# One encoder layer for two request groups on one core: a head by channel quarters, a gate in column tiles, a balance that paces the filler, and split weights kept in DRAM

## The chip, the cores and the metric

The kernel runs on one NeuronCore of a Trainium2 chip. The metric is the device time of one execution in microseconds; "the time" is the median of several executions. A profiled execution is one more, taken by the hardware profiler, and its trace is what the views below show. The engines are PE (TensorE, matmuls; PEld is its loading of weights), DVE (VectorE), ACT (ScalarE), POOL (GpSimd) and SP, which here issues all DMAs in order.

## What is computed

Two groups (prompt and sample) of 1024 tokens by 1024 channels go through the same layer with the same weights:

```python
mod = silu(c) @ w_ada + b_ada
shift, scale, gate = split(mod, 3)
h = rms_norm(x, norm_g) * (1 + scale) + shift
qa, ka, va, za, qb, kb, vb, zb, ga, gb = split(h @ w_in)
oa = gqa_attention(rope(rms_norm(qa)), rope(rms_norm(ka)), va) * silu(za)
ob = diff_attention(rope(rms_norm(qb)), rope(rms_norm(kb)), vb, lam)
ob = rms_norm(ob, subln_g) * (1 - lam_init) * silu(zb)
merged = sigmoid(ga) * (oa @ w_proj_a) + sigmoid(gb) * (ob @ w_proj_b)
y = x + gate * (merged @ w_out)
```

Branch A has 8 query heads on 2 key heads of 64; branch B has 4 heads with two 64-wide softmax maps each. Everything is float32.

## The kernel before

**Precision.** Most matmuls run in the fast float32r form. To keep accuracy each operand is split into a high part (a rounded copy, made by ACT) and a low part (the residual, made by DVE), and three products are summed: high-high, high-low, low-high. For a weight tile `split_w` (L175) does this, called by `load_w` (L186, lines L178 and L179 per quarter) and in `load_w_proj` (L220, L221). `load_w` brings a tile of 1024 x 256 in four DMAs of 256 KB into three rotating buffers and splits each into one of two weight buffers (`wpool`). Both groups load and split all 21 column tiles of `w_in` anew, 84 quarters per group.

**Head of group one.** `start` (L337) loads the adaLN weights (8 tiles of 1 MB, `load_ada`), x transposed in two halves of 512 tokens (`load_xT0`), and the weights of ka and va. `ada` (L292) multiplies the two conditioning vectors (2 columns as weights) with 512 columns of adaLN weights, 64 records of L298 in all; `ada_end` turns the result with small transposes into columns `modc`. `squares`, `added`, `inv_rms` and `spread` (L251 to L288) make the root-mean-square factors; `modulated` (L317) scales, shifts and splits x into `ht`, first for channels 0 to 3, then 4 to 7. `start_late` (L368) does the second half of the tokens. Then `head` (L1020) weaves `kva_gen` and `qa_gen` (projections through `proj_tt`, L506, 24 matmuls of 256 columns each at L515) with z steps.

**Fillers.** `z_gen` (L693) makes the gates of both branches and the merge gates: 12 items a group, each four tiles of 24 matmuls of 512 columns (L704), each tile three steps. Their result goes to DRAM (`zd`, L715). These steps depend on `ht` alone and fill TensorE while attention waits on other engines.

**Attention.** 32 units of branch A, then 16 of branch B, each for 256 queries: scores on PE (L737, L738), maximum on DVE (L739), exponential on ACT (L741), a flip by DVE's 32 x 32 transpose (L774) and four DMAs (L779), a split (L787, L788), and the product with the values (L799, L800 for A, L839 for B). For B the second map is scaled by a factor from a reciprocal (L760) on DVE and a product on POOL (L761). In `rows` (L523) the normalisation of q and k has a small addition on DVE (L532) and a power on POOL (L533).

**Order.** Python generators yield after each step, and `weave` (L71) runs several of them by shares: each stream has a number of steps and a lead, and the one whose done share less its lead is smallest goes next. `phase` (L1115) weaves one part of attention with the projections that the next part needs and with a fixed number of z steps (`Z_SHARE`, `ATT_W`, `IN_A`, `Z_A`, tables of constants). Tile's scheduler then fixes each engine's order with its own model of time, with attention at a raised priority; the kernel's engines run these orders.

**End of a group.** The last attention head (h = 3) is woven with `fill` (gate columns by `gate_gen`, L445, in group one; leftover z steps; part of `merge_gen`) and with `gated_gen` (L912), which multiplies attention by its gates and norm factors. For branch B the factors are spread by PE transposes of a broadcast column (L942). `merge_gen` (L954) projects both branches, `out_gen` (L992) makes the output; in group one the next group's `ht_gen` runs beside it.

Of the kernel before, what the change touches and what calls it, by code (L numbers as in the profile page):

```python
# [20 lines left out]
P = 128  # L21
# [15 lines left out]
Z_SHARE = (  # L37
    (7, 19, 6, 3, 2, 4),
    (9, 14, 7, 3, 2, 6),
)  # L40
Z_HEAD = (6, 5)
Z_HEAD_A = (-0.4, -0.45)
ATT_W = (
    (1.07, 0.933, 1.1, 0.95, 1.129, 1.52),
    (1.15, 1.354, 1.035, 1.196, 0.85, 1.069),
)
IN_A = (
    (0.1, -0.05, 0.2, 0.05, 0.15, 0.1),
    (0.1, -0.05, 0.45, 0.25, 0.15, 0.65),
)  # L50
Z_A = (
    (0.1, 0.0, 0.4, -0.05, -0.2, 0.0),
    (0.15, 0.05, 0.35, 0.15, -0.3, -0.2),
)
LAST_ATT = 44
LAST_FILL = 26
GATED_A = -0.3
TAIL = 5
TAIL_A = 0.3
LAG = 2  # L60

# [20 lines left out]
def drain(*gens):  # L82
    for g in gens:
        if g is not None:
            for _ in g:
                pass


@with_exitstack
def kernel(ctx: ExitStack, tc: tile.TileContext, t: dict):  # L90
# [26 lines left out]
    alone = [True]  # L117
    turn = [0]

    def gbank():  # L120
        turn[0] += 1
        if alone[0] and turn[0] % 5 in (0, 2):
            return sbank()[:, :512]
        return fbank()
# [33 lines left out]
    dma = nc.sync.dma_start  # L158
    x_sample = t["x_sample"][0]
# [12 lines left out]
    nc.vector.memset(nhalf, -0.5)  # L172


    def split_w(w, q, st):  # L175
        wh = w[:, q * 2 : q * 2 + 2, 0, :]
        wl = w[:, q * 2 : q * 2 + 2, 1, :]
# [3 lines left out]
    def split_early(what):  # L181
        w, sts = what
        for q, st in enumerate(sts):
            split_w(w, q, st)

    def load_w(pieces, early=False):  # L186

        w = wpool.tile([P, NCH, 2, 256], F32R, tag="w", name=nm("w"))
        sts = []
        for q in range(4):  # L190
            if early:
                if q % 2 == 0:
                    room = halves2(ptile())
                st = room[q % 2].rearrange("p (c n) -> p c n", c=2)
# [4 lines left out]
            for src in pieces(q):  # L199
                n = src.shape[1]  # L200
                dma(st[:, :, off : off + n], src.rearrange("(c p) n -> p c n", p=P))
# [4 lines left out]
        return (w, sts) if early else w  # L206

    def w_cols(mat, *cols):
        def pieces(q):
            return [mat[q * 256 : (q + 1) * 256, c : c + n] for c, n in cols]  # L210
        return pieces

    def load_w_proj(br, half):

        w = wpool.tile([P, 4, 2, 512], F32R, tag="w", name=nm("w"))
        mat = t["w_proj_b" if br else "w_proj_a"][0]
        for c in range(4):
# [3 lines left out]
            nc.vector.tensor_tensor(out=w[:, c, 1, :], in0=st, in1=w[:, c, 0, :].bitcast(F32), op=ALU.subtract)  # L221
        return w
# [990 lines left out]
```

## Time and profile before

| | |
|---|---|
| median of 3 runs | 1942.35 us (1939.26 to 1943.64) |
| the profiled execution's own time | 1933.24 us |
| its span, first to last instruction | 1931.5 us |
| PE / DVE / ACT / POOL busy | 1881.2 / 1397.3 / 991.7 / 414.7 us |
| DMA moved | 295.25 MB, mean 153 GB/s |

In the views, "PE" rows are matmuls, and float32 (not float32r) matmuls stand as two records each. A row of the timeline has start, length, engine, line, operation, tiles, shapes and count; in brackets stands the idle time before it with what ended it. In the rows of the stretches a number in brackets is a count. Rows of groups have busy us and the mean ns of one, then the idle time before them. PE's busy time is longer than its work where matmuls are not back to back, so a share near 100% does not mean full pace.

### The profile page before, as it was taken

To read this page: it belongs to the slowest core of one execution; us is meant where nothing else is said; L and a number is where in the kernel's file an instruction comes from. 1 tells how busy PE (TensorE), PEld (TensorE's weight loads), DVE (VectorE), ACT (ScalarE), POOL (GpSimd) and SP (SyncE) were. 2 spreads that over 40 slices of the span, in tenths; PEclk is the share of its full clock that TensorE was granted. 3 is DMA by queue.
4 is the path that set the end of the run, shared out by engine and by line. 5 is a ranking of instruction groups with operands and counts; after the bars stand their busy time and mean duration, and the time that the engine had idled before them with its cause. 6 is when DMAs were issued, how large, how long until landed. Compare 5 with 4: busy or idle time off the path is not lost.

```text
span 1931.5 us, 30797 instructions
## 1 busy us (share of the span) xinstructions
PE 1881.2 (97%) x10466; PEld 1610.0 (83%) x10466; DVE 1397.3 (72%) x2145; ACT 991.7 (51%) x2091; POOL 414.7 (21%) x758
## 2 busy tenths in 40 slices
PE   8899999999999999999999999999989999999999
PEld 3788888888988995778889888898877989888887
DVE  5669886778898677767465788688788767777731
ACT  4446665666666454414233566566666545542310
POOL 1342300120335051000124231013221524201000
PEclk9999999999999999999999999999999999999999
DMA  9125465556554436875641455565545343477522
GB/s 319 45 81 146 135 173 148 153 148 176 152 142 110 116 92 192 273 256 181 218 140 39 137 144 166 145 172 151 154 129 162 107 113 100 143 234 264 180 104 77
DMA packets 271613, 295.25 MB, mean 153 GB/s; under 512 B 37857, under 2 KB 220257, under 8 KB 271457
## 3 DMA queue, kind: packets, MB, share of 16 engines
q1 hardware_dynamic: 271456, 293.28, 51.4%
q8 instruction: 84, 1.38, 0.3%
q14 instruction: 73, 0.59, 0.1%
HBM read 133.72 MB, written 42.01 MB: 91 GB/s over the span
## 4 chain that ended last, share of the span: by engine, by line
PE 81%; DVE 7%; DMA 5%; issue 2%; ACT 2%; SPq 1%; POOL 1%; DVEq 0%; ACTq 0%; POOLq 0%
PE f L704 22%; PE f L515 19%; PE f L1007 5%; PE s L737 5%; PE a L839 5%; PE s L738 5%; PE f L976 4%; PE s L1007 4%; PE a L800 3%; PE a L799 3%; PE s L976 2%; DMA q<-p 2%; DVE m L739 2%; DVE p L774 1%; PE f L298 1%
## 5 line engine op out<-in xcount | busy, mean ns | idle before, releaser
L704 PE MATMUL f<-u,w 128*128 128x512 f32 x2232 | 574.2, 395 | 2.0 <-DVE ssB L863 1.5
L515 PE MATMUL f<-w,u 128*128 128x256 f32 x3456 | 487.5, 285 | 7.5 <-DVE u L571 3.7
L515 PEld LDWEIGHTS f<-w,u 128*128 128x128 f32 x3456 | 457.8, 190 | 29.0 <-DVE u L571 4.3
L704 PEld LDWEIGHTS f<-u,w 128*128 128x128 f32 x2232 | 404.2, 188 | 77.8 <-DVE ssB L863 1.8
L739 DVE TENSOR_REDUCE m<-s 128x1 f32<-128x1024 f32 x256 | 311.0, 1217 | 51.3 <-PE s L738 48.4
L774 DVE STREAM_TRANSPOSE p<-p 128x1024 f32<-128x1024 f32 x192 | 238.3, 1241 | 92.7 <-ACT p L741 89.3
L738 PE MATMUL s<-u,sw 128*128 128x512 f32 x512 | 203.8, 398 | 0.0
L788 DVE TENSOR_TENSOR q<-q,hi 128x512 fp32r<-128x512 f32 x256 | 171.5, 690 | 34.3 <-ACT hi L787 32.3
L787 ACT ACTIVATE hi<-q 128x512 fp32r<-128x512 f32 x256 | 153.6, 624 | 76.2 <-DMA q<-p 37.8
L741 ACT ACTIVATE p<-s,m,rsA 128x1024 f32<-128x1024 f32 x128 | 153.8, 1202 | 71.4 <-DMA q<-p 69.6
L178 ACT ACTIVATE w<-st 128x512 fp32r<-128x512 f32 x196 | 114.4, 625 | 99.2 <-DMA st<-in_w_in_dram 42.4
L741 ACT ACTIVATE p<-s,m,rsB 128x1024 f32<-128x1024 f32 x128 | 154.3, 1205 | 6.5 <-DMA q<-p 1.9
L179 DVE TENSOR_TENSOR w<-st,w 128x512 fp32r<-128x512 f32 x196 | 132.8, 706 | 34.2 <-ACT w L178 33.1
L658 POOL TENSOR_TENSOR row<-row,gB 128x96 f32<-128x96 f32 x64 | 33.8, 528 | 485.7 <-ACT row L529 474.1
L799 PE MATMUL a<-hi,u 128*128 128x256 f32 x512 | 132.2, 284 | 2.8 <-DMA q<-p 1.8
L800 PE MATMUL a<-q,u 128*128 128x256 f32 x512 | 129.3, 286 | 2.6 <-DVE q L788 2.6
L976 PE MATMUL f<-u,w 128*128 128x512 f32 x540 | 130.5, 393 | 1.3 <-DVE u L987 1.3
L839 PE MATMUL a<-q,u 128*128 128x256 f32 x512 | 127.1, 385 | 3.9 <-DVE oo L816 3.0
L976 PEld LDWEIGHTS f<-u,w 128*128 128x128 f32 x540 | 100.5, 188 | 23.0 <-DVE u L987 2.3
L839 PEld LDWEIGHTS a<-q,u 128*128 128x128 f32 x512 | 95.6, 193 | 20.0 <-DVE oo L816 3.6
L737 PE MATMUL s<-u 128*128 128x512 f32 x256 | 108.3, 424 | 3.3 <-ACT p L741 3.2
L737 PE MATMUL s<-u,u 128*128 128x512 f32 x256 | 102.4, 400 | 8.5 <-ACT p L741 3.1
(181 smaller groups left out, 2557.5 us busy)
## 6 DMA issues: line engine op xcount, KB each, us to landing
q<-p SPq DMA_DIRECT2D x768, 128.0 KB, 2.6
st<-in_w_in_dram SPq DMA_DIRECT2D x132, 256.0 KB, 3.1
zd<-ev SPq DMA_DIRECT2D x96, 256.0 KB, 2.2
sw<-u SPq DMA_DIRECT2D x256, 64.0 KB, 2.1
p<-zd SPq DMA_DIRECT2D x64, 256.0 KB, 3.7
u<-in_w_ada_dram SPq DMA_DIRECT2D x8, 1024.0 KB, 10.4
st<-in_w_in_dram SPq DMA_DIRECT2D x64, 128.0 KB, 2.8
st<-in_w_out_dram SPq DMA_DIRECT2D x32, 256.0 KB, 3.6
```

What stands on the lines that cost most here:

```text
L515: nc.tensor.matmul(ps, lt[c][:, sl], w[:, c, wi, :], start=(k == 0), stop=(k == 23))
L704: nc.tensor.matmul(ps, w[:, c, wi, e * P : (e + 1) * P], rt[c], start=(k == 0), stop=(k == 23),)
L737: nc.tensor.matmul(s[:, sl], q, k[:, sl], start=True, stop=False)
L738: nc.tensor.matmul(s[:, sl], sw, k[:, sl], start=False, stop=True)
L739: nc.vector.tensor_reduce(out=m, in_=s, axis=AX.X, op=ALU.max, negate=True)
L741: nc.scalar.activation(pt.rearrange("p (j c a) -> p j c a", j=4, c=8), s.rearrange("p (c a j) -> p j c a", c=8, j=4), AF.Exp, scale=rs, bi ...
L774: nc.vector.transpose(pt, pt)
L799: nc.tensor.matmul(acc, lt, th[:, c, :], start=(k == 0), stop=False)
L800: nc.tensor.matmul(acc, lt, tl[:, c, :], start=False, stop=(k == 7))
L839: nc.tensor.matmul(acc, u["v"][:, k], pT[:, k], start=(k == 0), stop=(k == 7))
L976: nc.tensor.matmul(ps, w[:, c, wi, d * P : (d + 1) * P], o[:, oi, :], start=(k == 0), stop=(k == 11))
L1007: nc.tensor.matmul(ps, w[:, c, wi, e * P : (e + 1) * P], m[:, mi, :], start=(k == 0), stop=(k == 23))
```

## The change

1. **Head by channel quarters.** x comes first; each adaLN tile pair holds shift and scale of 256 channels. `ada` uses four column positions of the array, 32 wide, one for each of four channel chunks, so that four partial sums stand in four strips of 32 partitions; `ada_sum` adds them with a small matmul. As soon as a quarter of the channels is modulated, its products for ka and va (`kva_early`) and for the first two z tiles (`z_one`) are accumulated, over the first 512 tokens, in four halves of PSUM banks and two banks that stay open. `act`, `vec`, `pe` and `dma_next` keep these instructions in the program's order. `z_first` goes on with four z tiles, the second half by chunks; `proj_tt` takes the finished tiles from `given`.
2. **Gate.** `gate_gen` works by four column tiles of 256, in the same strips, and stands behind the head's qa projection instead of in the last attention stretch.
3. **Pacing.** `phase` no longer weaves by shares. It keeps an account: each step has a cost on PE and on DVE, and the account grows by DVE's cost less PACE times PE's. At or below zero attention goes next; above it a projection step or a z step. No z shares are set per phase.
4. **Kept weights.** After group one has split a quarter of a `w_in` tile, `keep` stores high and low parts to DRAM (512 KB), and group two loads them with `again` straight into the weight buffer. `w_proj_a` likewise; `w_proj_b` and `w_out` are split as before.
5. **Small moves.** The addition at L532 goes to POOL; the reciprocal at L760 becomes a power on POOL; the copy at L855 goes to ACT; branch B's norm factors go through DRAM (`rB`) and come back broadcast, instead of by PE transposes.
6. **Constants** for the head and the last stretch (`Z_HEAD`, `LAST_ATT`, `LAST_FILL`, `TAIL` and their leads).

```diff
+PACE = (
+    (1.15, 0.95, 1.0, 1.0, 1.0),
+    (0.95, 0.95, 1.05, 1.0, 1.02),
+)
+EARLY = (
+    (1.2, 1.05, 1.35, 1.22, 1.22),
+    (1.2, 1.1, 1.2, 1.23, 1.15),
+)
+A_STEP, B_STEP, F_STEP, Z_STEP = (0.47, 1.01), (0.68, 0.98), (0.79, 0.65), (1.82, 0.35)
...
+    def keep(key, q, w):
+
+        kept[key, q] = dpool.tile([P, 1024], F32, name=nm("kept"))
+        dma(kept[key, q].rearrange("p (c s n) -> p c s n", c=2, s=2), w[q].bitcast(F32))
+
+    def again(key, q, w):
+        dma(w[q].bitcast(F32), kept[key, q].rearrange("p (c s n) -> p c s n", c=2, s=2))
...
         for q in range(4):
+            if (key, q) in kept:
+                again(key, q, w)
+                continue
...
             if not early:
                 split_w(w, q, st)
-        return (w, sts) if early else w
+                if pieces.of is w_in:
+                    keep(key, q, w)
...
+    def ada(wts, cpad):
+
+        acc = gbank()
+        for q, wt in enumerate(wts):
+            for c in range(4):
+                pe.matmul(
+                    acc[32 * c : 32 * c + 32], cpad[:, q * 4 + c], wt[:, c], start=(q == 0), stop=(q == 1),
+                    tile_position=(0, 32 * c),
+                )
...
+        rs = inv_rms(added(squares(xT[0])))
...
+        rsb = spread(rs)
+        early.update(kva=[x for b in two_banks() for x in (b[:, :256], b[:, 256:])], z=two_banks())
+        ps = ada_sum(ada(wts[:2], cpad))
+        for quarter in range(4):
+            cs = range(quarter * 2, quarter * 2 + 2)
+            by_rms(xT[0], cs, rsb)
+            split_early(kva_w[0][1], quarter)
+            ada_end(quarter, ps)
...
+            split_early(kva_w[1][1], quarter, act)
+            modulated(ht, 0, xT[0], cs)
+            split_early(kva_w[1][1], quarter, vec)
+            for c in cs:
+                kva_early(ht, c)
+            part = ada(wts[quarter * 2 + 2 : quarter * 2 + 4], cpad) if quarter < 3 else None
+            for c in cs:
+                for e in range(2):
+                    z_one(ht, 0, c, kva_w[1][0], e, early["z"][e], pe)
...
     def gate_gen():
...
+        for n in range(4):
+            acc = gbank()[:, :256]
+            nc.vector.memset(acc, 0.0)
...
+                        nc.tensor.matmul(
+                            acc[32 * c : 32 * c + 2], cT[:, q * 4 + c], st[:, j], start=(q == 0), stop=(q == 1),
+                            tile_position=(0, 32 * c),
+                        )
...
-        nc.vector.tensor_scalar(out=ss, in0=ss, scalar1=EPS, scalar2=None, op0=ALU.add)
+        nc.gpsimd.tensor_scalar(out=ss, in0=ss, scalar1=EPS, scalar2=1.0, op0=ALU.add, op1=ALU.mult)
...
-            nc.vector.reciprocal(f, su)
+            nc.gpsimd.tensor_tensor(out=f, in0=su, in1=mone, op=ALU.pow)
...
-        nc.vector.tensor_copy(query_order(o), piece_order(acc))
+        nc.scalar.activation(query_order(o), piece_order(acc), AF.Copy)
...
-                rb = gbank()
-                for k in range(4):
-                    r = st["ssB"][:, e - 4, hf * 4 + k : hf * 4 + k + 1]
-                    nc.tensor.transpose(rb[:, k * P : (k + 1) * P], r.to_broadcast([P, P]), ident)
+                dma(rb, rB[e % 2, hf].partition_broadcast(P))
...
+            drain(islice(zs, 6))
+            late()
+            weave((kva, 27, 0.0), (islice(zs, Z_FIRST[0]), Z_FIRST[0], Z_FIRST_A[0]))
+            weave((qa, 27, 0.0), (islice(zs, Z_FIRST[1]), Z_FIRST[1], Z_FIRST_A[1]), (gate_gen(), 8, GATE_A))
...
+        def phase(k, *fs):
+
+            n_att, att_cost = (16 * (6 + PV_LAG), A_STEP) if k < 2 else (4 * (9 + PV_LAG), B_STEP)
+            fs, n_fs = chain(*fs), 31 * len(fs)
+            done, seen, live, fs_live, z_live = 0, 0, True, True, True
+            while live or fs_live:
+                cost = None
+                if live and ahead[0] <= 0.0:
+                    live = next(att) is None
+                    seen += 1
+                    cost = att_cost if live else (0.0, 0.0)
+                elif fs_live and (not live or not z_live or done * n_att < n_fs * EARLY[g][k] * seen):
+                    fs_live = next(fs, None) is not None
+                    done += 1
+                    cost = F_STEP
+                elif z_live:
+                    z_live = next(zs, None) is not None
+                    cost = Z_STEP
+                else:
+                    live = live and next(att) is None
+                    seen += 1
+                    cost = att_cost
+                ahead[0] += cost[1] - PACE[g][k] * cost[0]
...
-            if g == 0:
-                yield from gate_gen()
             yield from zs
             drain(first)
-            yield from islice(merge, 16 - TAIL)
+            yield from islice(merge, 16 - TAIL[g])
```

More of the change, by code (lines that the diff above doesn't have):

```diff
@@ L117 @@
     alone = [True]
+    early = {}
     turn = [0]
@@ L121, in gbank @@
         turn[0] += 1
-        if alone[0] and turn[0] % 5 in (0, 2):
+        if alone[0] and not early and turn[0] % 5 in (0, 2):
             return sbank()[:, :512]
@@ L1040, in new_state @@
         st["rA"] = dpool.tile([64, P], F32, name=nm("rA"))
+        st["rB"] = [dpool.tile([16, P], F32, name=nm("rB")) for _ in range(2)]
         st["od"] = [
```

379 lines of the change are left out of this document (219 added, 160 removed).

## The prediction, as it was put down

> **What bounds the kernel now.** I read the page's busy shares and chain first, then the busy time by stretch, then the chain in order of time for the pace of single matmuls.
>
> ```profile
> span 1931.5 us, 30797 instructions
> PE 1881.2 (97%) x10466; PEld 1610.0 (83%) x10466; DVE 1397.3 (72%) x2145; ACT 991.7 (51%) x2091; POOL 414.7 (21%) x758
> PE 81%; DVE 7%; DMA 5%; issue 2%; ACT 2%; SPq 1%; POOL 1%; DVEq 0%; ACTq 0%; POOLq 0%
> ```
>
> TensorE is the bound: 81% of the chain. So I ask two things: how much TensorE work goes, and where TensorE waits. By stretch (columns: stretch and its length, then busy us and count of PE, PEld, DVE, ACT, POOL, granted clock, DMA share, GB/s):
>
> ```profile
> 0.00:41.80 41.80, 34.09 (x102) 9.12 (x102) 19.84 (x35) 17.19 (x29) 5.36 (x10) 1.00 1.00 357
> 41.80:139.60 97.80, 88.38 (x591) 81.23 (x591) 63.35 (x174) 44.34 (x115) 36.50 (x58) 0.97 0.22 62
> 139.60:740.00 600.40, 594.87 (x3542) 526.36 (x3541) 475.69 (x666) 372.93 (x788) 155.64 (x298) 1.00 0.51 141
> 740.00:850.00 110.00, 103.93 (x442) 74.67 (x441) 80.21 (x116) 42.01 (x81) 6.47 (x14) 1.00 0.80 257
> 1405.00:1445.00 40.00, 32.99 (x183) 28.06 (x182) 30.66 (x41) 24.38 (x51) 6.88 (x14) 0.91 0.46 126
> 1480.00:1490.00 10.00, 6.45 (x20) 4.86 (x19) 7.28 (x9) 4.20 (x9) 0.34 (x1) 0.66 0.49 135
> ```
>
> The long attention stretch of group one idles 5.5 of 600 us: nothing to win there. Idle time sits in the head (7.7 and 9.4 us), at the end of group one's attention (6.1), and at two phase changes of group two (7.0 and 3.6). What one matmul takes when nothing stops it is read from unbroken pieces of the chain (start, us, what):
>
> ```profile
> 17.30 3.52 PE s L298 x8
> 119.35 2.87 PE f L515 x24
> 626.15 3.45 PE a L839 x16
> 858.32 0.44 PE f L942 x4
> 902.10 5.44 PE f L976 x24
> ```
>
> So 512 columns in fp32r take 0.227 us, 256 take 0.120, an adaLN or gate record 0.44, one transpose 0.11. With these paces "busy" can be checked: busy in the head is not full pace.
>
> **The head.** The first projection starts at 41.88 and attention's first score at 138.57:
>
> ```profile
> 6.85 9.21 PE L298 MATMUL f<-u,cT 128*2 128x512 f32 x16 [6.85 <-DMA u<-in_w_ada_dram]
> 41.88 1.70 PE L515 MATMUL f<-w,u 128*128 128x256 f32 x12
> 138.57 0.50 PE L737 MATMUL s<-u,u 128*128 128x512 f32 x1 [2.84 <-DVE ev L712]
> 41.80:139.60 97.80, 50.57 (x384) 48.55 (x384) 0.97 0.22 62
> 41.80:139.60 97.80, 32.22 (x120) 22.74 (x120) 0.97 0.22 62
> ```
>
> The last two rows are the same stretch for L515 alone and L704 alone: 384 x 0.120 + 120 x 0.227 = 73 us of projections in 97 us. Before 41.88 TensorE does only the 64 adaLN records (64 x 0.44 = 28 us) while DMA is full.
>
> The change loads x's first half, then two adaLN tiles, two weights, six adaLN tiles: 12.6 MB, 35 us at the 357 GB/s of the first stretch, so about 36.5 us. Each channel quarter is then modulated and used at once. Its work, from these rows:
>
> ```profile
> 10.71 2.43 ACT L254 ACTIVATE q<-u 128x512 f32<-128x512 f32 x4 [8.15 <-DMA u<-in_xT_prompt_dram]
> 14.54 1.23 DVE L260 TENSOR_TENSOR q<-q,q 128x1024 f32<-128x1024 f32 x1 [4.90 <-ACT q L254]
> 23.65 0.69 DVE L179 TENSOR_TENSOR w<-p,w 128x512 fp32r<-128x512 f32 x1 [1.64 <-ACT w L178]
> 22.38 1.03 POOL L278 TENSOR_TENSOR rs<-ss,nhalf 128x4 f32<-128x4 f32 x1
> 35.79 0.99 DVE L323 TENSOR_SCALAR u<-u,modc 128x512 f32<-128x512 f32 x2
> 37.30 2.48 DVE L327 TENSOR_TENSOR u<-u,u 128x512 fp32r<-128x512 f32 x4
> 66.10 5.73 DVE L374 SCALAR_TENSOR_TENSOR u<-u,modc,ev 128x512 f32<-128x512 f32 x8 [2.16 <-ACT ev L287]
> ```
>
> Two scalings (1.4), two modulations (1.0), two residuals (1.3), two weight residuals (1.4) and small ones (0.6) make about 5.7 us a quarter. x lands near 7; squares (4.9), adds (3 x 1.23 + 0.69 = 4.4) and the root's way through PE, DVE, POOL's power (1.03), PE and ACT (about 4, an estimate) put the start at 20, so DVE ends the fourth quarter near 43, as the last adaLN tile does (36.5, then its own 4 and a quarter's tail). TensorE has then done 96 x 0.120 + 48 x 0.227 = 22 us, ends near 45, where the old kernel has begun 3 us ago. (Behind each of these steps PE's next one waits in order, z behind the next quarter's adaLN tile: that is in the 45.) Next come two z tiles over the first half (48 x 0.227 = 11 us, to 56) while the second half's norm runs: x at 42, ready near 55 against 66.10 today. Then z and kva of the second half (33 us), qa with five z steps and the gate (23 + 9 + 4): 56 + 69 = 125, and 6 us for weight changes and the waits that the stretch shows today: **first score at 131**. By then 232 z matmuls are issued instead of 144; 24 of the 144 came late today, so I count 208 against 120: 88 x 0.227 = 20 us of filler no longer needed later. Gain 7.6 + 20, **28 us**; bounds 12 (a round of DVE, ACT and PE adds 4 us a quarter) and 36 (no waits at all).
>
> This takes the adaLN records at a quarter of their time, 7 us. Their four tiles sit at four column positions and write four disjoint strips, 16 per position. No row shows tiled matmuls: bounds are 28 us (nearest row, L298) and 7. I take the lower, since otherwise four instructions of 32 columns would keep the whole array, and make the upper a rival. The Trainium skill (TensorE: Matmul & The Clock Gate, Part 3) gives 2.38 times for three column tiles; by that, the estimate for these records would be 9 to 12 us. Against the change speaks TensorEngine Tiling, Key Properties, in the Trainium skill: changing the tiling mode drains the engine; no run here shows it, and some 25 changes would have to cost 1 us each to matter.
>
> **The gate.** Out of the last attention stretch of group one goes this:
>
> ```profile
> 733.30 2.67 PE f L452 x6
> 742.89 4.38 DMA st<-in_w_ada_dram
> 755.08 3.35 DMA st<-in_w_ada_dram
> ```
>
> 32 x 0.445 = 14 us of work, and 7.7 us of loads on the chain. The new gate lies behind the head's qa, its 4 us counted above. In a stretch that is 94% busy I take **11 us**; bounds 0 (attention's own chain ends last: DVE 80 of 110 us) and 18.
>
> **Branch B's norm factors** go through DRAM: 64 transposes of 0.11 us leave, 7 us; the round trip is covered by merge matmuls (12 x 0.227 = 2.7 us each). I take **5 us**; if the cover fails, two waits like the existing one on rA:
>
> ```profile
> 759.90 4.11 DMA tab<-rA
> ```
>
> cost 8 us, 1 more than is saved. Behind a load that waits for these factors stand the next tile's loads of o and z on SP's queue, and merge waits for those.
>
> **Kept weights.** In group two 84 of the 96 splits after 998 us go:
>
> ```profile
> L179 DVE TENSOR_TENSOR w<-st,w 128x512 fp32r<-128x512 f32 x96 | 64.2, 698 | 16.3 <-ACT w L178 15.8
> L178 ACT ACTIVATE w<-st 128x512 fp32r<-128x512 f32 x96 | 56.0, 625 | 60.2 <-PE s L1007 16.7 <-PE f L1007 16.6 <-DMA st<-in_w_in_dram 16.2
> ```
>
> That is 58 us of DVE and 53 of ACT, on engines that are not the bound. It pays only where attention is late: the two phase changes, 10.6 us idle in all. With the pacing by balance, which keeps z steps for such places, I take **6 us** of them; bounds 0 and 14 (with the slow pace beside them). The price: 84 stores of 512 KB in group one on SP's queue, and 84 loads twice as big in group two. SP's rows (min/median/max ns), what it waits for, and landing:
>
> ```profile
> L779 SPq DMA_DIRECT2D q<-p x768: 542/602/1844, 144.1 to 1762.2; - x192
> L594 SPq DMA_DIRECT2D sw<-u x256: 461/594/1964, 109.8 to 1708.1; - x128
> L715 SPq DMA_DIRECT2D zd<-ev x96: 325/529/648, 63.4 to 1744.0; - x96
> L201 SPq DMA_DIRECT2D st<-in_w_in_dram x196: 367/419/3488, 35.0 to 1670.9; - x196
> SPq L201 <- DVE w L179: 95.9, 58, 21.7
> st<-in_w_in_dram SPq DMA_DIRECT2D x132, 256.0 KB, 3.1
> ```
>
> A store like zd's takes 0.53 us of SP: 84 make 44 us in a 600 us stretch in which SP issues half of these rows, 374 us, 62%. Behind each stand flips (L779) and swaps (L594), for which attention waits. I take **+4 us** (a tenth of the 44); bounds 0 and the slower rival's.
>
> **Small moves.** 64 reciprocals and 112 additions go to POOL, 32 copies to ACT, which the page shows at 21% and 51%; TensorE's filler hides them.
>
> ```profile
> L533 POOL TENSOR_TENSOR rs<-ss,nhalf 128x2 f32<-128x2 f32 x16 | 11.6, 726 | 48.7 <-DVE ss L532 46.7 <-PE f L515 2.0
> L760 DVE RECIPROCAL r<-su 128x1 f32<-128x1 f32 x64 | 10.1, 158 | 28.7 <-ACT p L741 28.1
> ```
>
> A power costs at most 0.73 instead of 0.16 us, so up to 64 x 0.57 = 36 us on the flips' chain if that cover is gone: **+1 us**, bounds 0 and 36.
>
> **Pacing elsewhere** can only equal 5.5 us idle in 600: 0, with the rival below for a loss. Sum: -28 - 11 - 5 - 6 + 4 + 1 = -45 us. The profiled execution took 1933.24 us (span 1931.5 and 1.7 around it), so 1888.2; the median of the runs shown, 1942.35, is 1.0047 times that one: **1897 us**.
>
> **Rivals.**
> - *Everything works*: head 36, gate 18, factors 7, group two 14, no costs: -75, (1933.24 - 75) x 1.0047 = 1867 us. For: each is a bound above. Against: all at once. Chance 0.15.
> - *Column tiles don't overlap*: adaLN keeps 28 us (+21) in the quarters, which then are TensorE's 50 us, and the gate 14 (+11): -13, 1929 us. For: L298 costs 0.44 with 2 weight columns. Against: DMA covers part. Chance 0.12.
> - *Group two waits for its weights*: a load starts only when its tile is free, and must land: 21 loads x (3.1 + 0.42) - 21 splits x 1.32 = +46, and the 6 us are gone: +7, 1949 us. Against: TensorE has scores and a second stream meanwhile. Chance 0.10, of which 0.02 faster, 0.04 within, 0.04 slower.
> - *SP becomes attention's bound in group one*, slower: each store occupies SP 0.53 us and holds it until its split is done (95.9/58 = 1.65 us a wait): 84 x 2.18 = 183 us in front of flips. SP is free 38% of the time, so up to 62%, 113 us, can reach TensorE. At half of that, 57 us: -45 - 4 + 57 = +8, 1950 us; fully, 2007. It decides from 53 us on, 0.63 us a store. For: SP already stands on the chain. Against: stretch 139.6 to 740 idles 1%. Chance 0.15.
>
> **How the numbers follow.** Forecast 0.48, with its own range 1880 to 1915. Range for all: 1862 to 1955, which leaves out what lies beyond the best case's own figure and the last rival's far half. About 0.2% is what a measurement here can tell from no change. Faster: 0.48 + 0.15 + 0.12 + 0.02 = 0.77; within 0.04; slower 0.04 + 0.15 = 0.19.
>
> **What would show it.** Right: projections before 26 us, first score near 131, adaLN records starting four at a time, no gate rows after 700, L179's count down by 84, no 7 us idle at group two's phase changes. Wrong: a first score after 138, SP waiting on splits with DVE's flips late in group one, TensorE idle at each weight change after 998. The forecast fails most simply if the balance spends z steps early and branch B's phases then run at DVE's pace.

## The result and the profile after

The changed kernel takes **1955.87 us** (median of 5 runs, 1950.74 to 1958.73), against 1942.35 (1939.26 to 1943.64) for the kernel before: ratio 1.007, 95% interval 1.0052 to 1.0087. It is slower by 0.7%. I had put 0.77 on faster, with 1897 us.

The profiled execution took 1956.09 us, at its median; that of before, 1933.24, lies 9 us under its median. So the traces stand 22 us apart and the medians 13.5, and a difference of a few microseconds in one stretch says nothing.

The page of the changed kernel: span, busy times, chain, and what the kept weights move (last column: us from issue to landing).

```profile
span 1953.9 us, 30637 instructions
PE 1867.9 (96%) x10406; PEld 1608.0 (82%) x10406; DVE 1313.6 (67%) x1875; ACT 950.2 (49%) x2027; POOL 456.6 (23%) x932
PE 64%; DMA 12%; DVE 10%; SPq 6%; ACT 4%; issue 3%; POOL 1%; ACTq 0%; DVEq 0%
w<-kept SPq DMA_DIRECT2D x84, 512.0 KB, 5.9
kept<-w SPq DMA_DIRECT2D x80, 512.0 KB, 4.1
```

Every engine that the change meant to relieve is relieved: PE by 13 us of busy time, DVE by 84, ACT by 42. But TensorE's share of the chain fell from 81 to 64%, and flips, their issue and VectorE took its place. The work is less and the waiting more. Where, is read by stretch: the head up to the first row maximum of attention, group one's attention up to its last row maximum, the passage to group two's first, group two's attention, and the end. First before, then after (columns as in the prediction).

```profile
0.00:139.60 139.60, 122.47 (x690) 90.36 (x691) 83.19 (x209) 61.52 (x144) 41.86 (x68) 0.98 0.45 150
139.60:809.60 670.00, 659.98 (x3804) 569.51 (x3803) 527.68 (x737) 405.12 (x850) 159.85 (x307) 1.00 0.54 151
809.60:1076.40 266.80, 265.22 (x1384) 226.91 (x1383) 169.72 (x324) 87.70 (x190) 49.64 (x71) 1.00 0.52 173
1076.40:1750.80 674.40, 657.34 (x3804) 578.37 (x3803) 530.58 (x743) 406.54 (x856) 159.35 (x307) 0.99 0.53 148
```

```profile
0.00:185.90 185.90, 154.53 (x901) 121.74 (x901) 97.45 (x236) 64.17 (x145) 41.13 (x82) 0.95 0.63 205
185.90:844.80 658.90, 625.79 (x3613) 547.53 (x3612) 509.44 (x646) 406.67 (x861) 183.19 (x378) 0.98 0.69 201
844.80:1113.60 268.80, 266.83 (x1375) 228.03 (x1375) 149.16 (x280) 73.86 (x169) 54.00 (x88) 1.00 0.59 201
1113.60:1776.70 663.10, 647.61 (x3758) 567.95 (x3757) 473.27 (x586) 374.37 (x798) 174.06 (x378) 1.00 0.63 181
```

The head is 46 us longer, group one's attention 11 shorter, the passage 2 longer, group two's attention 11 shorter, the end 4 shorter: 22 in all. Now the z matmuls of group one's attention, before and then after (PE and PEld busy, clock, DMA share, GB/s):

```profile
139.60:809.60 670.00, 264.78 (x1020) 183.98 (x1021) 1.00 0.54 151
```

```profile
185.90:844.80 658.90, 218.87 (x864) 157.18 (x864) 0.98 0.69 201
```

156 matmuls fewer at 0.227 are 35 us, and the gate's 14 are gone too: some **50 us of TensorE work left this stretch, and it became 11 us shorter**. The rest turned into idle time (1.5% of the stretch before, 5% after) and into a lower clock (0.98 instead of 1.00). So there are two questions: why is the head so long, and why did attention not give the time back?

**The head.** TensorE's rows in time (start, length; f<-u,at are the adaLN records, s<-w,u the products for ka and va, s<-u,w the z tiles):

```profile
17.34 3.56 PE L92 MATMUL f<-u,at 128*32 128x512 f32 x16
23.99 0.72 PE L92 MATMUL s<-w,u 128*128 128x256 f32 x2 [1.31 <-ACT u L92]
36.22 0.46 PE L92 MATMUL s<-w,u 128*128 128x256 f32 x2
37.49 2.90 PE L92 MATMUL s<-w,u 128*128 128x256 f32 x22 [0.81 <-DVE u L92]
40.32 1.92 PE L92 MATMUL f<-u,at 128*32 128x512 f32 x16
45.96 0.46 PE L92 MATMUL s<-w,u 128*128 128x256 f32 x2
57.08 0.50 PE L92 MATMUL s<-w,u 128*128 128x256 f32 x2 [1.26 <-ACT u L92]
63.97 3.42 PE L92 MATMUL s<-u,w 128*128 128x512 f32 x12
131.68 0.61 PE L549 MATMUL f<-st,cT 128*2 128x256 f32 x8
182.91 0.47 PE L868 MATMUL s<-u,u 128*128 128x512 f32 x1 [3.12 <-DVE u L673]
```

The quarters begin at 23.99, 36.22, 45.96 and 57.08, and the last ends at 67.4: about 10.9 us each, where I had 5.7. The first score comes at 182.91, where I had 131. The column tiles do what they should in the last two of the four adaLN tiles: 16 records in 1.92 us, 0.12 each against 0.44 before (the first two take 3.56 and 2.21). The gate's do so at their best, 8 records in 0.61 us; most stand four at a time in 0.60. In the first and the last quarter 22 products take 5.06 us instead of 2.90: the granted clock was 0.51 and 0.58 there. These two stretches with all engines, then the gate's 64 records alone:

```profile
24.00:30.30 6.30, 5.71 (x26) 5.20 (x26) 4.17 (x7) 0.64 (x1) 0.00 (x0) 0.51 1.10 348
57.10:64.00 6.90, 5.37 (x25) 5.17 (x26) 5.32 (x8) 1.67 (x3) 0.00 (x0) 0.58 0.25 93
0.00:185.90 185.90, 7.66 (x64) 1.35 (x64) 0.95 0.63 205
```

**The change from branch A to branch B in group one.** Of attention's idle time the largest piece lies here. All engines of the changed kernel, then its z matmuls alone:

```profile
560.00:570.00 10.00, 7.30 (x50) 6.47 (x49) 9.72 (x15) 8.33 (x18) 5.19 (x13) 1.00 0.47 111
570.00:580.00 10.00, 6.21 (x28) 4.53 (x27) 6.36 (x8) 5.61 (x13) 4.26 (x10) 0.85 0.60 141
580.00:590.00 10.00, 8.55 (x29) 5.91 (x27) 9.82 (x11) 6.43 (x13) 1.08 (x3) 0.64 0.34 79
```

```profile
570.00:580.00 10.00, 0.00 (x0) 0.00 (x0) 0.85 0.60 141
```

From 570 on TensorE does only attention's own matmuls, waits between them, and gets 0.64 of its clock right after. How they wait for one another is seen in single rows:

```profile
573.60 5.46 SPq L910 DMA_DIRECT2D q<-p  x7
576.62 1.21 ACT L872 ACTIVATE p<-s,m,rsB 128x1024 f32<-128x1024 f32 x1 [2.55 <-DMA q<-p]
577.97 0.80 PE L868 MATMUL s<-u 128*128 128x512 f32 x1 [1.84 <-ACT p L872]
578.56 0.63 PE L869 MATMUL s<-u,sw 128*128 128x512 f32 x1
578.99 0.63 PE L868 MATMUL s<-u 128*128 128x512 f32 x1
580.08 1.23 DVE L870 TENSOR_REDUCE m<-s 128x1 f32<-128x1024 f32 x1 [3.48 <-PE s L869]
```

Flips hold up ScalarE's next exponential, that one holds the next scores, and these hold VectorE's next maximum. VectorE, 97% busy from 560 to 570, is 64% busy in the next 10 us.

### The profile page after: what moved, and what is told of

Its sections match the earlier page's. It is cut to its first block, busy times and chain, and to the rows that moved or that the text cites. A ratio compares the mean times of both kernels' runs of the same rounds, so it can differ in the third digit from the quotient of the medians.

```text
span 1953.9 us, 30637 instructions
## 1 busy us (share of the span) xinstructions
PE 1867.9 (96%) x10406; PEld 1608.0 (82%) x10406; DVE 1313.6 (67%) x1875; ACT 950.2 (49%) x2027; POOL 456.6 (23%) x932
## 2 busy tenths in 40 slices
DMA packets 277307, 371.82 MB, mean 190 GB/s; under 512 B 39392, under 2 KB 208544, under 8 KB 276128
## 4 chain that ended last, share of the span: by engine, by line
PE 64%; DMA 12%; DVE 10%; SPq 6%; ACT 4%; issue 3%; POOL 1%; ACTq 0%; DVEq 0%
PE f L617 15%; PE f L841 13%; PE f L1143 6%; PE f L1112 5%; DMA q<-p 5%; SPq L910 4%; PE a L970 4%; PE s L868 4%; PE s L869 3%; PE s L1143 3%; DVE m L870 3%; PE s L1112 2%; ACT p L872 2%; DMA row<-zd 2%; DVE p L905 2%
## 5 line engine op out<-in xcount | busy, mean ns | idle before, releaser
L841 PE MATMUL f<-u,w 128*128 128x512 f32 x2016 | 510.7, 394 | 7.8 <-DMA w<-kept 3.4
L617 PE MATMUL f<-w,u 128*128 128x256 f32 x3360 | 469.7, 286 | 4.6 <-DVE u L673 3.0
L617 PEld LDWEIGHTS f<-w,u 128*128 128x128 f32 x3360 | 441.5, 192 | 25.8 <-issue 6.2
L841 PEld LDWEIGHTS f<-u,w 128*128 128x128 f32 x2016 | 366.7, 188 | 80.6 <-DMA w<-kept 5.1
L761 POOL TENSOR_TENSOR row<-row,gB 128x96 f32<-128x96 f32 x64 | 26.8, 420 | 469.8 <-ACT row L631 469.5
L1112 PE MATMUL f<-u,w 128*128 128x512 f32 x540 | 129.5, 393 | 2.0 <-DVE u L1123 1.3
L1112 PEld LDWEIGHTS f<-u,w 128*128 128x128 f32 x540 | 100.9, 188 | 24.4 <-DVE u L1123 2.1
L1143 PE MATMUL f<-u,w 128*128 128x512 f32 x480 | 111.2, 389 | 0.0
L904 DVE SCALAR_TENSOR_TENSOR p<-p,r,p 128x1024 f32<-128x1024 f32 x64 | 83.6, 1306 | 40.7 <-POOL r L892 36.3
```

The costliest lines, as they stand in the source:

```text
L617: nc.tensor.matmul(ps, lt[c][:, sl], w[c][:, wi, :], start=(k == 0), stop=(k == 23))
L841: nc.tensor.matmul(ps, w[c][:, wi, e * P : (e + 1) * P], rt[c], start=(k == 0), stop=(k == 23),)
L1112: nc.tensor.matmul(ps, w[:, c, wi, d * P : (d + 1) * P], o[:, oi, :], start=(k == 0), stop=(k == 11))
L1143: nc.tensor.matmul(ps, w[c][:, wi, e * P : (e + 1) * P], m[:, mi, :], start=(k == 0), stop=(k == 23))
```

## The experiments

All ratios are to the kernel before, run beside each on the same chip; the changed kernel itself stands at 1.007.

**The head.** First the stores that SP issues ahead of x's second half. SP's rows of the changed kernel:

```profile
36.73 8.22 SPq L195 DMA_DIRECT2D kept<-w  x5
45.00 3.66 SPq L92 DMA_DIRECT2D u<-in_xT_prompt_dram  x4
49.02 13.21 SPq L195 DMA_DIRECT2D kept<-w  x3
62.28 0.43 SPq L92 DMA_DIRECT2D st<-in_w_in_dram  x1
```

*head_no_store*: the head's 12 stores are left out, and group two splits these three tiles again (and stores them then, 12 stores before its attention begins).

```diff
-                if pieces.of is w_in:
+                if pieces.of is w_in and room is None:
                     keep(key, q, w)
...
-        for _, (w, _), key in kva_w:
-            for q in range(4):
-                keep(key, q, w)
```

> Only the twelve stores of the head's three weights are left out (group two splits these three again). If the stores in SP's order ahead of x's second half and between the loads of the third weight delay the head: x's second half is issued before 38 us, not 45, the third weight's four loads stand together, first score near 160 to 168, time 1932 to 1942. If the chain of the quarters is the cause, the first score moves by less than 6 us and the time by less than 8.

*x_early*: the same, and x's second half is loaded right behind the adaLN tiles.

```diff
         wts += [load_ada(n) for n in range(2, 8)]
+        xT.append(load_xT0(1))
...
-        xT.append(load_xT0(1))
```

> As the one before, and x's second half is loaded right behind the adaLN tiles. If SP's order is the whole of the head's loss, the second half is normalised before the fourth quarter ends and the first score falls to about 145 to 155, time 1915 to 1930. If the quarters' chain is the bound, projections of the first half still end near 60 to 67 us, and the gain over the one before is under 8 us.

*chain_break*: x_early with another order inside a quarter.

```diff
-            for c in cs:
-                kva_early(ht, c)
             part = ada(wts[quarter * 2 + 2 : quarter * 2 + 4], cpad) if quarter < 3 else None
+            for c in cs:
+                kva_early(ht, c)
+                if part is not None:
+                    ps, part = ada_sum(part), None
...
-                if part is not None:
-                    ps, part = ada_sum(part), None
```

> The changed kernel without the head's kept stores, x's second half loaded right behind the adaLN tiles (as in x_early, 1964.55 us, first score 177 us), and the order of one quarter turned: TensorE does the next quarter's adaLN tile ahead of this quarter's projections and its sum behind the first chunk's projections. If the long quarters (about 10 us instead of 5.7) come from a chain in program order TensorE, ScalarE, TensorE, VectorE, ScalarE, VectorE, TensorE: the first half of the head ends 10 to 15 us sooner, first score near 165, time near 1952. If the head is late because TensorE has that much more work in front of the first score, the quarters may shorten but the first score stays at 174 to 178 and the time at 1960 to 1966.

Measured: 1956.85 (1.0086, 1.0068 to 1.0105), 1964.55 (1.0117, 1.0096 to 1.0139) and 1967.21 (1.013, 1.011 to 1.015). The first score comes at 173.9, 173.6 and 177.2 us: the stores cost the head 9 us; the earlier load of x gains nothing beyond that, and the other order inside a quarter nothing at all. (The 177 us that the last expectation gives for x_early is its first row maximum.) And the 9 us did not reach the end: by the traces, group two's attention is 6, 12 and 18 us longer than in the changed kernel. Why breaking the chain did not help is in TensorE's rows of chain_break:

```profile
40.05 1.92 PE L92 MATMUL f<-u,at 128*32 128x512 f32 x16
41.90 1.70 PE L92 MATMUL s<-w,u 128*128 128x256 f32 x12
44.32 1.05 PE L92 MATMUL f<-two,row 128*128 128x2 f32 x8 [0.72 <-ACT row L92]
45.24 1.68 PE L92 MATMUL s<-w,u 128*128 128x256 f32 x12
46.75 2.91 PE L92 MATMUL s<-u,w 128*128 128x512 f32 x12
49.59 1.93 PE L92 MATMUL f<-u,at 128*32 128x512 f32 x16
```

One quarter takes 9.5 us, from 40.05 to 49.59, with a single gap of 0.72. The rest, **8.8 us**, is TensorE's own work (the five rows add up to 9.3, since each ends a little behind the start of the next). The chain through four engines, my second theory, was not the cause here: TensorE is.

**Kept weights**, taken out of the changed kernel and put into the kernel before.

```diff
-                if pieces.of is w_in:
-                    keep(key, q, w)
...
-        if not br:
+        if False:
             kept[br, half] = [dpool.tile([P, 2048], F32, name=nm("kept")) for _ in range(2)]
```

> The changed kernel with no weights kept in DRAM: no stores in group one, group two splits its weights again. If the stores and the bigger loads are what costs (on SP's queue in the head, and on the DMA engines in attention), the first score comes near 160 instead of 183 us and the whole falls by 20 to 35 us, to about 1920 to 1935. If the head is late because each quarter is one chain through PE, ACT and DVE, and the pacing loses the rest, the first score stays above 172 and the time stays above 1940; without the DVE and ACT relief in group two it may even rise.

*before_keep*, in `load_w` of the kernel before (80 quarters; the first tile of the head is split in both groups):

```diff
+            if (key, q) in kept:
+                dma(wq, kept[key, q].rearrange("p (c s n) -> p c s n", c=2, s=2))
+                continue
...
                 split_w(w, q, st)
+                if pieces.of is w_in:
+                    kept[key, q] = dpool.tile([P, 1024], F32, name=nm("kept"))
+                    dma(kept[key, q].rearrange("p (c s n) -> p c s n", c=2, s=2), wq)
```

> The kernel before with kept weights alone (80 quarters stored in group one, loaded in group two; its first weight stays out). If SP and traffic make kept weights a loss: 15 to 40 us slower, 1957 to 1982, most of it in group one's attention. If they are harmless: within 8 us of 1942, and where they help at group two's phase changes (11 us idle before) down to 1930.

Measured: without them 1974.18 (1.0183, 1.0161 to 1.0205); in the kernel before 1976.54 (1.0184, 1.0159 to 1.0208). Both are worse, by some 20 and 36 us. Group two's attention without them, and then in head_no_store and chain_break, where all weights of this stretch are loaded as in the changed kernel:

```profile
1109.50:1795.00 685.50, 654.35 (x3761) 574.74 (x3760) 519.71 (x663) 411.55 (x871) 183.94 (x378) 0.99 0.56 149
1108.80:1777.60 668.80, 649.49 (x3758) 570.44 (x3758) 471.82 (x587) 375.05 (x800) 178.27 (x378) 0.99 0.62 180
1108.40:1789.40 681.00, 655.27 (x3758) 573.89 (x3757) 471.91 (x588) 375.87 (x800) 177.16 (x378) 0.98 0.61 177
```

Without them it is 22 us longer than with them (663.1), while group one's attention, where the 84 stores are, is no shorter: 662.6 us without, 658.9 with. So in the changed kernel the stores cost attention nothing that shows. Whether the loads pay is not shown: chain_break loads them too, VectorE has 472 us of work as in the changed kernel (473), and the stretch is 18 us longer all the same. In the kernel before, the same part makes group one's attention 13.5 us longer and group two's 12. The passage takes 16 more. One part with opposite signs in two kernels: that was the first hint that what a part seems to cost depends on the order it stands in.

**Parts alone in the kernel before.** *gate_alone*: the gate in column tiles, behind the head's qa. *small_alone*: norm factors through DRAM, and the small moves.

```diff
-LAST_FILL = 26
+LAST_FILL = (18, 26)
...
-            weave((chain(kva, qa), 40, 0.0), (islice(zs, nz - 6), nz - 6, Z_HEAD_A[g]))
+            weave((chain(kva, qa), 40, 0.0), (islice(zs, nz - 6), nz - 6, Z_HEAD_A[g]), (gate_gen(), 16, -0.45))
...
-                yield from gate_gen()
```

> The kernel before with one part of the change: the gate by column tiles, behind the head's second projection instead of at the end of group one's attention. By the prediction's term: 11 us less, 1929 us; the last stretch of group one shorter by 15 to 18 us and the head longer by 4 to 8. By its lower bound (attention's own chain ends last there): 1938 to 1942, with the head's cost showing.

```diff
-            nc.vector.reciprocal(f, su)
+            nc.gpsimd.tensor_tensor(out=f, in0=su, in1=mone, op=ALU.pow)
...
-                    nc.tensor.transpose(rb[:, k * P : (k + 1) * P], r.to_broadcast([P, P]), ident)
+                dma(rb, rB[e % 2, hf].partition_broadcast(P))
```

> The kernel before with branch B's norm factors through DRAM and the small moves (reciprocal and epsilon to GpSimd, the copy of the output piece to ScalarE). By the prediction's terms: 5 less and 1 more, 1936 us. If the factors' round trip is not covered: 1941 or more, with TensorE idle at the start of branch B's merge. If the power on GpSimd lies on the flips' chain: 1945 or more, lost in the stretches of branch B's attention.

*no_gate*: the kernel leaves out the gate, so its output is not the layer's. It is no part of the change but the cleanest removal of TensorE work. As in gate_alone, the last stretch of group one is woven for 18 steps of filler instead of 26.

```diff
-LAST_FILL = 26
+LAST_FILL = (18, 26)
...
             if g == 0:
-                yield from gate_gen()
+                nc.vector.memset(gatec, 0.5)
```

> The kernel before with the gate's columns left out altogether (the gate becomes a constant; 14 us of TensorE work, 4 MB of loads and their wait leave the end of group one's attention; nothing is added anywhere). If TensorE's work sets the time there: 14 to 18 us less, 1923 to 1927, all of it in group one's last attention stretch (73.2 us before). If the attention's own chain (VectorE, ScalarE, flips) is next in line: that stretch shrinks by 8 to 9 us as in gate_alone, 1932. If each stream's constants fit only the order that they were made for: the stretch shrinks, but other stretches grow and the time is at or above 1940.

Measured: 1991.64 (1.0258, 1.0238 to 1.0277), 1964.47 (1.0118, 1.0097 to 1.014) and 1950.53 (1.0037, 1.0019 to 1.0055; medians of 10 runs and 19 of before). All three slower, even the one that only leaves work out. In the last stretch of group one's attention, where the gate was, the time falls as predicted: 73.2 us before, 65.1 in the changed kernel, 64.4 and 63.2 in gate_alone and no_gate. But the stretch ahead of it grows, from 74.4 us to 79.7, 77.9 and 77.8, and before_keep, whose gate stands where it stood before (26 of its 32 records in the last stretch), looks the same: 80.1 us and then 64.4. Its gate records in that last stretch:

```profile
762.80:827.20 64.40, 12.78 (x26) 1.37 (x26) 1.00 0.79 248
```

So both stretches together gain 3 to 7 us where the gate is gone and 3 where it stays. In gate_alone the five phases ahead of the last stretch, whose constants nobody touched, grew from 596.8 to 623.8 us (between the same row maxima), and in no_gate the passage and group two's attention, which run the same instructions in another order, took 271.1 and 683.2 us instead of 266.8 and 674.4.

**The order alone.** So I changed one constant and no instruction. *nudge* moves the lead of the head's z steps, *nudge_att* one weight of group one's second phase, both in the kernel before; *nudge_after* one constant of the balance.

```diff
-Z_HEAD_A = (-0.4, -0.45)
+Z_HEAD_A = (-0.36, -0.45)
```

> The kernel before with one constant of the head moved by a tenth (the lead of the z steps, -0.4 to -0.36): same instructions, another order. If an order is only worth what its work and waits are worth, the time stays within 4 us of 1940. If the time depends on an order found by trial, it goes up by 10 us or more, in stretches that the constant does not belong to, and single parts of the change cannot be priced by putting them into the kernel before.

```diff
-    (1.07, 0.933, 1.1, 0.95, 1.129, 1.52),
+    (1.07, 0.95, 1.1, 0.95, 1.129, 1.52),
```

> The kernel before with one weight of the second phase moved by a fiftieth (0.933 to 0.95): same instructions, some 300 of 10065 matmuls in another place. If one order is as good as its neighbours: within 4 us of 1942. If the constants were found by trial and their neighbours are worse: 5 to 15 us more, as in nudge (+0.6%).

```diff
-    (1.15, 0.95, 1.0, 1.0, 1.0),
+    (1.15, 0.95, 0.98, 1.0, 1.0),
```

> The changed kernel with one constant of the balance moved by a fiftieth (third phase of group one, 1.0 to 0.98): same instructions, some 350 of 9993 matmuls in another place. If the changed kernel's constants are less well fitted, this is as likely to gain as to lose: 1945 to 1965. If they are fitted as well as those of before: 5 to 15 us more, 1960 to 1970. If order matters little: within 4 us of 1956.

Measured: nudge 1953.78 (1.0058, 1.004 to 1.0077), nudge_att 1948.12 (1.0033, 1.0019 to 1.0047), nudge_after 1969.88 (1.0142, 1.0116 to 1.0168, 14 us above the changed kernel). **The same instructions in a slightly different order cost 10, 6 and 14 us**, and TensorE's share of the chain falls from 81% to 72 and 74% in the first two. Where they lose it, the traces tell less sharply than the medians: that of nudge lies 6 us above its median, that of before 9 below, and no_gate, which has TensorE's order of before up to 728 us, comes to the change from A to B 4.6 us later. But one place stands out. The phase after the change from A to B in the kernel before, in nudge and in nudge_att:

```profile
513.50:578.50 65.00, 63.93 (x387) 56.56 (x386) 60.65 (x92) 44.71 (x99) 24.22 (x51) 1.00 0.53 145
```

```profile
524.60:595.40 70.80, 64.58 (x355) 55.87 (x354) 60.67 (x90) 44.87 (x98) 19.30 (x41) 0.93 0.53 142
```

```profile
519.30:588.80 69.50, 64.31 (x367) 55.28 (x366) 60.89 (x90) 45.02 (x98) 20.01 (x42) 0.98 0.53 144
```

VectorE and ScalarE do the same in all three; TensorE does 20 to 32 matmuls less in a longer stretch, at a lower clock. In the kernel before TensorE idles 1.1 us of this phase, in every other order that I ran 5 to 17, except in no_gate's, which is the same up to there. It is only a part of the loss: 5.8 of 19.5 us that nudge loses in group one's attention (7.8 are in the first phase) and 4.5 of 8.7 in nudge_att. nudge_after loses in the two phases behind it (84.7 and 85.0 us instead of 76.5 and 79.7).

**Is it filler in the wrong place?** Stepping through the account with its constants gives group one's third phase 6 z steps, where the shares of before had 18. Four kernels move z steps or projections between places of the changed kernel, and a fifth puts the shares back.

*hold_filler* (`PACE`) and *even_proj* (`EARLY`), each in group one's row:

```diff
-    (1.15, 0.95, 1.0, 1.0, 1.0),
+    (1.15, 1.05, 0.9, 1.0, 1.0),
...
-    (1.2, 1.05, 1.35, 1.22, 1.22),
+    (1.2, 1.05, 1.0, 1.22, 1.22),
```

> The changed kernel with two constants of the balance moved: fewer z steps in the second phase of group one (0.95 to 1.05) and more in the third, where attention changes from branch A to branch B (1.0 to 0.9). If the loss at that change (no z and no projection matmul from 570 to 590 us, TensorE at 0.74 of its clock) is filler spent too early, TensorE loses less than 8 us instead of 19.5 there and the time falls by 8 to 15 us, to 1941 to 1948. If the chain of attention is the bound there whatever fills TensorE, the stretch keeps its length and the time is 1952 to 1960.

> The changed kernel with one constant moved: the projections of group one's third phase come at the pace of attention (1.35 to 1.0) instead of ahead of it. If projections spent too early leave the change from A to B bare, the 72 projection matmuls of 550 to 570 us spread over it, and the time falls by 5 to 10 us, to 1946 to 1951. If attention there waits for those projections (its queries and keys), it gets longer: 1960 to 1970.

*filler_back*, and *filler_half* with (20, 4):

```diff
-Z_FIRST = (22, 7)
+Z_FIRST = (18, 0)
```

> The changed kernel with 11 z steps (11/3 x 24 x 0.227 = 20 us of TensorE) given back from the head to group one's attention; the head keeps only the z steps that its open banks need. If attention there is held by its own chain while TensorE idles (61 us lost in group one's attention, against 22 before), the first score comes 15 to 20 us sooner (166), attention grows by less than 10, and the time is 1940 to 1947. If TensorE's work sets attention's time, it grows by the same 20 us and the time stays at 1952 to 1960. If the order matters most, anything up to 1985.

> The same with 5 of these 11 steps given back (9 us of TensorE). By the chain: first score near 175, time 1946 to 1951. By TensorE's work: 1952 to 1960. By the order: anything, and not between filler_back and the changed kernel.

*old_pace*, with the other tables as they were before:

```diff
+Z_SHARE = (
+    (7, 17, 5, 3, 2),
+    (9, 14, 7, 3, 2),
+)
```

> The changed kernel with the old pacing by shares and weights in the six phases (shares lowered for the z steps that the head already did), all else as changed. If the balance of two engines' time puts the filler in the wrong places, the 19.5 us lost in group one's fourth phase and the 12 us in its second go back to below 8 together, and the time falls by 15 us or more, to 1940 or less. If the balance is not what costs, the old weights, which were made for another mix, are as good or worse: 1955 to 1975.

Measured: hold_filler 1985.31 (1.0219, 1.0179 to 1.0258), even_proj 1970.02 (1.0132, 1.0099 to 1.0164), filler_back 1991.47 (1.0255, 1.0228 to 1.0282), filler_half 1990.64 (1.0254, 1.0225 to 1.0284), old_pace 2037.92 (1.0497, 1.0474 to 1.0519). None helps. filler_back did not ask what I meant to ask: the account places the same number of z steps in each phase whatever is left, so the 11 steps went to the end of group one's attention and the passage (296.7 us instead of 268.8). Two more kernels therefore put steps at the change itself: *back_at_change* is filler_back with the constant below, *fill_change* the changed kernel with 0.85 in its place.

```diff
-    (1.15, 0.95, 1.0, 1.0, 1.0),
+    (1.15, 0.95, 0.8, 1.0, 1.0),
```

> filler_back put its 11 z steps into the last stretch (28 left there instead of 17), since the account places the same number in each phase. Here the account's constant for group one's third phase, where attention changes from A to B, goes from 1.0 to 0.8 as well: that phase gets 18 z steps instead of 6 (before had 18), 17 are left as in the changed kernel, and the head keeps what filler_back keeps. If TensorE idles at the change because its filler is elsewhere, third and fourth phase together lose less than 15 us instead of 36 (17.0 and 19.5) and the time is 1935 to 1955. If attention there is late for its own reasons, the phase grows by the 22 us of filler and the time is 1965 to 1995.

> The changed kernel with that constant alone, 1.0 to 0.85: 14 z steps in the third phase instead of 6, 8 fewer left for the last stretch of group one. If the idle time at the change can take filler: 15 us of work leave the last stretch and nothing is added at the change, 1940 to 1948. If not: 1955 to 1975.

Measured: 1993.87 (1.0253, 1.0212 to 1.0294) and 1974.22 (1.0167, 1.0129 to 1.0205). back_at_change around the change, all engines and then its z matmuls:

```profile
541.00:644.50 103.50, 86.39 (x415) 71.66 (x414) 76.58 (x96) 58.89 (x125) 21.55 (x45) 0.87 0.61 171
```

```profile
541.00:644.50 103.50, 22.32 (x91) 16.32 (x90) 0.87 0.61 171
```

Now 91 z matmuls stand there, and TensorE still idles 17 of 103 us at 0.87 of its clock. Group one's second and third phase take 280.3 us against 258.5 in filler_back: 21.8 more, and 12 steps of 8 x 0.227 are 21.8. The filler's time was simply added here, and taken off the passage, which is 27 us shorter (269.3 us). fill_change shows that taking filler out need not pay: its last stretch has 71 z matmuls less than that of the changed kernel (16 us), and with the passage it is 6 us longer (340.1 instead of 333.9). As I read these runs, filler that stands at a fixed place of an in-order queue does not flow into the gaps: it stands in front of attention's next matmul or behind it, and the gaps stay.

## Why the prediction was wrong, point by point

- **What bounds the kernel: right as a reading, wrong as a price.** TensorE was on 81% of the chain, so I priced TensorE work taken out of a busy stretch at a microsecond for each (20 for filler moved to the head) or little less (11 for the gate). This is the step that failed most: 50 us left group one's attention and 11 came back. no_gate shows it with almost none of the rest: 14 us of work gone, and the time up by 0.4%. Some 22 us more were lost in the head, which is 46 us longer for an estimated 24 us of added work (35 of z and 8 of gate, less 19 of adaLN). Attention's stages follow one another in fixed orders on five queues; as I read it, a stretch that is 99% busy was one whose order fitted its work, not one with spare speed behind TensorE.
- **First score at 131: wrong by 52 us.** 22 of them came in the quarters (67.4 instead of 45). I took VectorE's 5.7 us as a quarter's length. TensorE's own list was longer: 22 us of products and 7 of adaLN over four quarters are already 7.3 a quarter, and both stood in my text. Besides, the sums of the strips (1 us a quarter) were not counted: 8.8 us measured in chain_break, and TensorE is busy for 9.0 of 9.8 us in the changed kernel's second quarter. By estimate 11 of the 22 us are this list (9.0 a quarter, where 20 to 45 leaves 6.2), 4 the later start (24 instead of 20) and 4 the low clock of the first and the last quarter; the rest is waits. The other 30: I counted 232 z matmuls up to there, and 288 run, 13 us more; 9 are the kept stores ahead of x's second half (head_no_store), which I had priced only for attention; some 8 are idle time that I did not trace to one cause.
- **Column tiles: right**, 9.6 us for the 64 records, 7.7 at the pace of the last two tiles, against 28, and that rival is dead. I saw no drain at a change of tiling mode, which the Trainium skill (TensorEngine Tiling, Key Properties) states: in chain_break the rows at 40.05 and 41.90 follow each other with no idle time.
- **The gate: its 11 us are not shown.** The last stretch is 8 to 10 us shorter, but the one ahead of it is 3 to 5 longer, and before_keep has the same shift with the gate in place. In the head it keeps TensorE busy for 7.7 us, where I had 4.
- **Kept weights: not settled.** Without them group two's attention is 22 us longer, against my 6, but chain_break loses 18 us there and keeps them. The +4 for SP's stores, and the rival that SP becomes attention's bound, did not show: group one's attention is not shorter without the stores. Nor did group two wait for its weights: TensorE's waits for them add up to 3.9 us, and its attention got shorter.
- **Norm factors and small moves:** not told apart; together in the kernel before +1.2%. Whether that is their own cost or the order's no run shows.
- **Pacing elsewhere at 0: wrong.** My warning, that the balance spends z steps early and branch B then runs bare, described the picture at 570 us well. As a cause it fell: with z steps put back there the idle time stayed.
- **What I had no term for** is that a new order of the same work costs 6 to 14 us here. Part of the loss at the change from A to B may be this, since every order but that of before idles there. How much of the 13.5 us a longer search of constants for the changed kernel would win back stays open, as does which single wait starts each gap. No kernel of mine beats the one before.

## What to carry to other kernels

Before pricing TensorE work taken out of a busy stretch, ask what the other engines would do in the time saved: if they too follow fixed orders, the gain is what the next chain allows, and it may be nothing. Where the order is made by a planner from constants found by trial, move one constant by a few per cent first and see how far the time moves; parts whose price is below that cannot be judged one by one, and a change has to be weighed with its constants fitted anew. When work is cut into pieces that several engines handle in turn, add up every engine's list for one piece before naming its bound.

## What the runs showed of the hardware

- Four column strips of 32, each with its own two-column vector, ran 16 records of 512 columns in 1.92 us (two adaLN tiles of four), against 16 x 0.44 = 7.0 untiled: 3.7 times faster.
- Short waits can be paid twice. In the changed kernel TensorE waited 1.21, 0.70, 1.09 and 1.84 us between 568 and 578 us, and score matmuls of 512 columns then started 0.43 us apart (578.56, 578.99) instead of 0.23, until about 587. The granted clock was 0.64 from 580 to 590. It is no rule: from 390 to 430 TensorE idled 4.5 of 40 us, and the clock stayed at 1.00.
- 84 loads of 512 KB from DRAM into a weight buffer landed in 5.9 us (median), the 80 stores of the same size in 4.1. With 371.82 MB moved in all instead of 295.25, the flips' median landing went from 2.6 to 2.8 us.
